# A hybrid decoder layer in float32: the first gate and up pair of each half step done by two plain k groups and seven products

## The chip, the cores and the metric

One core of one Trainium2 chip. The metric is the device time of one execution in microseconds (us), here the median of three runs. Engines: PE (TensorE, matmuls), ACT (ScalarE), DVE (VectorE), POOL (GpSimd) and SP (SyncE, which issues most loads).

## The reference, cut to what matters

One layer on x of 256 tokens x 2048 channels. The two SwiGLU half steps, with which the change deals, are its first and its last part:

```python
x = x + 0.5 * swiglu(rms_norm(x, ffn1_norm[l]), ffn1_w_gate[l], ffn1_w_up[l], ffn1_w_down[l])
x = x + hybrid_mixer(rms_norm(x, mix_norm[l]), ...)
x = x + cross_attention(rms_norm(x, xattn_norm[l]), ...)
x = x + 0.5 * swiglu(rms_norm(x, ffn2_norm[l]), ffn2_w_gate[l], ffn2_w_up[l], ffn2_w_down[l])

def swiglu(h, w_gate, w_up, w_down):
    return (jax.nn.silu(h @ w_gate) * (h @ w_up)) @ w_down
```

w_gate and w_up are 2048 x 5632, w_down is 5632 x 2048, all float32.

## The kernel before, in words

**Numbers.** A float32 matmul is done as three with operands in a reduced float32 form: a value is split into a high part (a cast, on ACT) and a low part (value less high part, on DVE), and high x high, high x low and low x high are added up in PSUM. `split` (L144) does it; `wsplit` does it for weights and keeps the casts, and the low halves, in the order in which they are written.

**Tiles.** Tokens are two tiles (TT) of 128, each the stationary operand of a matmul. A k group is 512 rows of a weight matrix by 512 columns: a raw tile [128, 4, 512] of 1 MB, which `load` (L130) has SP fetch into one of a few places (tag "raw", in a pool `wp` and in the phase's own pool), and from which `wgroup` (L151) makes the split tiles wh and wl. A gate or up column block f (eleven of 512 columns) has four k groups over the 2048 channels: 24 matmuls of 128 x 512 for each group and matrix, in `mm3` (L170) or `whole` (L179). The normed x stands transposed and split in xT[0] to xT[3], one for each k group. The norm's factor r is applied behind the products.

**Seven products.** `strassen` (L223) takes two k groups (a, b), the two token tiles and a pair of matrices (gate and up, or two column blocks of down) and does their eight block products (`product`, L213, twelve matmuls each) as seven. For it DVE adds raw weights (`raw`, L237), a DMA on POOL's queue adds others in memory (L241, accumulating), the sums of x blocks sh and sl are made once by `sums_of` (L198: six steps on DVE in tiles fa and fb, then the split), and the products x and y, made in PSUM, are carried over into accumulators by an ACT copy (L254) and two DVE subtractions (L264, L269). The products in order, with a and b of the k groups, are: x from the left raw a; y from left a less right a (sh, sl); x again with another sum; c0l from the left b; x; c0r; and, behind or inside the whole groups, the seventh from x's second tile.

**A half step** is `ffn` (L374): the eleven f in three parts (4, 4 and 3). For each f the gate and up products, silu on ACT (sg, L420), h on DVE (L428), and, two ticks later, `turn` (L378): four PE transposes (tp, L383) for each token tile and the split of h into hTh (ACT) and hTl (DVE, L303). After a part its rows of w_down, by `strassen` over the part's first two h groups and whole groups for the rest, and x is updated (L442). For f = 0 both matrices are done plainly: `proj` (L288) runs gate over four groups, then up over four; the sums of xT[0] and xT[1] are made behind that. From f = 1 on `strassen` takes k groups 0 and 1 and `whole` does 2 and 3.

**At the start** three raw groups (gate 0, 1, 2) are loaded with x's transposed blocks xr; `first` (L481) multiplies these by the norm's gain (ACT for the first block, POOL for the others, L325), splits them into xTh and xTl. At the end of a half step `norm_chunk` (L334) makes the next phase's operands from each updated block of x: one tick later eight transposes (L343), the multiplication by the gain (xg, L345) and the split (L348, L349).

**What sets the order.** A scheduler gives each engine a fixed order by priorities (`tc.high_priority`, WPRI for weights) ahead of the run; `later` and `tick` (L89 to L100) place transposes a number of products later. Tiles live in pools by tag; a tile whose tag has n places waits for the release of the one n before it. A phase's pool is opened by `open_phase` (L64) and released at the end: half step 1, middle, half step 2. wh and wl have FWB = 3 places of a whole group in a half step and WB = 4 of half a group in the middle.

Of the kernel before, what the change touches and what calls it, by code (L numbers as in the profile page):

```python
# [8 lines left out]
F32 = mybir.dt.float32  # L9
# [7 lines left out]
P = 128  # L17
# [12 lines left out]
WB = 4  # L30
# [19 lines left out]
def layer_kernel(ctx: ExitStack, tc: tile.TileContext, A: dict, out: bass.AP):  # L50
# [65 lines left out]
    with tc.high_priority(100000):  # L116
        SY.dma_start(gain, A["gains"])
        for g in range(3):
            raw = wp.tile([P, 4, 512], F32, tag="raw", name="raw")
            wload.append(raw)  # L120
            step = 2 if g else 1
            xr = FT("h", 8, [P, 4, S], F32, "xr")
            xload.append(xr)
            for k in range(0, 4, step):
                SY.dma_start(xr[:, k:k + step], A["xT"][g, :, k:k + step])
                SY.dma_start(raw[:, k:k + step], A["ffn1_w_gate"][0, g, :, k:k + step])
    xs = [con.tile([P, TT, 512], F32, name=f"x{c}") for c in range(NC)]
# [22 lines left out]

    def wgroup(W, c, g, fine=None):  # L151
# [70 lines left out]

    def strassen(Wl, cl, Wr, cr, lhs, ab, sums, groups, mid=None, last=False):  # L223

# [26 lines left out]
        c0l, c0r, c1r = (pa.tile([P, 512], F32, tag="acc", name="acc") for _ in range(3))  # L251
        product(x, of(a, 0), parts(ral), True)
        with tc.high_priority(WPRI):
            SC.copy(c0l, x)  # L254
        add(ral, ral, rar)
# [6 lines left out]
        product(x, s_(1), parts(ral), False)  # L262
        with tc.high_priority(WPRI):
            V.tensor_sub(c0r, ys, x)  # L264
# [3 lines left out]
        with tc.high_priority(WPRI):  # L268
            V.tensor_sub(c1r, ys, x)  # L269
# [17 lines left out]

    def proj(W, c, lhs, groups, fine=None):  # L288

# [3 lines left out]
        for i, g in enumerate(groups):  # L293
            if fine and i:
                fine(4 * i)
            for h, half in enumerate(wgroup(W, c, g, fine if i == 0 else None)):
# [37 lines left out]
    def norm_chunk(c, src, g0, ss):  # L334
# [15 lines left out]

        later(1, turn)

# [21 lines left out]
    def ffn(pre, r, after, fine=None, last=False):  # L374
# [18 lines left out]
        for part in PARTS:  # L393
# [13 lines left out]
            for f in part:  # L407
                plain = sums is None
                if plain:
                    gate = proj(wg, f, lhs_x, range(4), fine)  # L410
                    if callable(r):
                        r = r()
                else:
                    gate, upv = strassen(wg, f, wu, f, lhs_x, (0, 1), sums, (2, 3),
                                         mid=sums_h if f == part[-1] else None)
                sg = []
# [5 lines left out]
                if plain:  # L422
                    upv = proj(wu, f, lhs_x, range(4))
                hs = []
                with tc.high_priority(WPRI):
                    for t in range(TT):
# [3 lines left out]
                later(2, lambda f=f, hs=hs: turn(f, hs))  # L430
                if plain:
                    with tc.high_priority(WPRI):
                        sums = sums_of(xT[0], xT[1])
                    kept = [tc.dram_tile([P, 2, 4, S], F32, name=f"{pre}_{n}") for n in ("sh", "sl")]
# [647 lines left out]
```

## Time and profile before

| | |
|---|---|
| median of three runs | 1919.73 us (1919.63 to 1920.5) |
| profiled execution | 1920.29 us |
| its span | 1918.5 us, granted clock 0.995 |
| matmuls and transposes | 8616 |
| PE, weight loads, DVE, ACT, POOL busy | 99%, 81%, 76%, 56%, 7% |
| memory read over the span | 379.10 MB |

In rows of waits stand total us, times and the longest wait. In rows of a timeline stand the start, the length, engine, line, operation, out<-in, the count of instructions merged, and in brackets the idle time before it with what ended it. In rows of groups stand the count, total us busy, mean ns of one and idle time before. "acc<-wh,xTh" is a matmul of the split weight and the split x into the accumulator acc.

### The profile page before, as it was taken

How to read it: one execution, taken by the hardware profiler on the slowest of the kernel's cores; microseconds unless marked ns; L12 is line 12 of the kernel's file. 1: busy time of each engine (PE TensorE's matmuls, PEld its weight loads, DVE VectorE, ACT ScalarE, POOL GpSimd, SP SyncE). 2: the span in 40 equal slices, each digit the busy share in tenths (PEclk: the TensorE clock that was granted, in tenths of full speed). 3: DMA queues.
4: the chain of work that ended last, by engine and by line, in shares of the span. 5: the costliest groups of instructions: out<-in, count | busy, mean ns of one | idle time of the engine just before them, and what ended most of it. 6: DMA issues, size and time to landing. Idle time of an engine off the chain costs nothing.

```text
span 1918.5 us, 21566 instructions
## 1 busy us (share of the span) xinstructions
PE 1890.5 (99%) x8616; PEld 1563.4 (81%) x8616; DVE 1459.3 (76%) x1159; ACT 1080.1 (56%) x1028; POOL 125.7 (7%) x137
## 2 busy tenths in 40 slices
PE   8999999999999999999999999899999999999998
PEld 6888888888888778778888889788888888888876
DVE  7779887788888885446785555777888878888886
ACT  6556655555555556444676445555655556556553
POOL 2000000000000000002230000000000000000000
PEclk9999999999999999999999999899999999999999
DMA  9776787777877754445465554668768777787775
GB/s 376 274 244 225 241 301 280 275 240 241 277 246 274 250 157 174 169 158 194 174 221 200 195 193 157 254 198 293 231 230 285 259 275 272 246 284 233 242 253 171
DMA packets 68480, 453.90 MB, mean 237 GB/s; under 512 B 7675, under 2 KB 8827, under 8 KB 15004
## 3 DMA queue, kind: packets, MB, share of 16 engines
q1 hardware_dynamic: 56284, 370.74, 49.2%
q0 software_dynamic: 10944, 79.70, 18.5%
q10 hardware_dynamic: 1152, 2.10, 0.3%
q8 instruction: 67, 1.10, 0.2%
q14 instruction: 33, 0.27, 0.0%
HBM read 379.10 MB, written 6.29 MB: 201 GB/s over the span
## 4 chain that ended last, share of the span: by engine, by line
PE 93%; DVE 4%; issue 1%; ACT 1%; DMA 1%; POOL 0%; SPq 0%; DVEq 0%; POOLq 0%; ACTq 0%
PE acc L184 24%; PE x L219 17%; PE acc L176 9%; PE acc L177 9%; PE acc L175 9%; PE acc L219 9%; PE x L184 8%; PE y L219 4%; DVE wl L145 2%; ACT wh L145 1%; PE tp L383 1%; DVE raw L237 1%; DMA xr<-in_xT_dram 0%; DMA raw<-raw 0%; PE tp L343 0%
## 5 line engine op out<-in xcount | busy, mean ns | idle before, releaser
L145 DVE TENSOR_TENSOR wl<-raw,wh 128x2048 fp32r<-128x2048 f32 (+2 forms) x523 | 1013.6, 1954 | 367.1 <-ACT wh L145 366.7
L145 ACT CAST wh<-raw 128x2048 fp32r<-128x2048 f32 (+2 forms) x523 | 852.2, 1640 | 621.3 <-DVE raw L237 182.2
L175 PE MATMUL acc<-wh,xTh 128*128 128x512 f32 x544 | 216.3, 399 | 9.0 <-ACT wh L145 8.8
L176 PE MATMUL acc<-wl,xTh 128*128 128x512 f32 x544 | 214.9, 395 | 4.6 <-DVE wl L145 4.6
L177 PE MATMUL acc<-wh,xTl 128*128 128x512 f32 x544 | 214.2, 394 | 0.0
L237 DVE TENSOR_TENSOR raw<-raw 128x2048 f32<-128x2048 f32 x64 | 146.5, 2290 | 1.7
L241 POOL DMA_DIRECT2D raw<-raw x64 | 55.0, 860 | 1201.2 <-ACT sg L420 473.8
L175 PEld LDWEIGHTS acc<-wh,xTh 128*128 128x128 f32 x544 | 103.1, 190 | 32.4 <-ACT wh L145 10.5
L176 PEld LDWEIGHTS acc<-wl,xTh 128*128 128x128 f32 x544 | 103.6, 190 | 28.0 <-DVE wl L145 6.9
L184 PE MATMUL acc<-wl,xTh 128*128 128x512 f32 x480 | 121.8, 389 | 0.0
L184 PE MATMUL acc<-wh,xTl 128*128 128x512 f32 x480 | 121.8, 389 | 0.0
L184 PE MATMUL acc<-wh,xTh 128*128 128x512 f32 x480 | 121.8, 389 | 0.0
L177 PEld LDWEIGHTS acc<-wh,xTl 128*128 128x128 f32 x544 | 103.6, 190 | 21.7
L184 PEld LDWEIGHTS acc<-wl,xTh 128*128 128x128 f32 x480 | 90.1, 188 | 18.7
L184 PEld LDWEIGHTS acc<-wh,xTh 128*128 128x128 f32 x480 | 90.1, 188 | 18.7
L184 PEld LDWEIGHTS acc<-wh,xTl 128*128 128x128 f32 x480 | 90.1, 188 | 18.7
L219 PE MATMUL x<-wh,sh 128*128 128x512 f32 x256 | 71.2, 400 | 3.3 <-ACT wh L145 1.9
L219 PE MATMUL x<-wh,sl 128*128 128x512 f32 x256 | 68.8, 390 | 0.0
L219 PE MATMUL x<-wl,sh 128*128 128x512 f32 x256 | 68.7, 390 | 0.0
L420 ACT ACTIVATE sg<-acc,r 128x512 f32<-128x512 f32 x24 | 16.3, 689 | 84.7 <-PE acc L184 84.7
L184 PE MATMUL acc<-wh,hTl 128*128 128x512 f32 x232 | 59.2, 390 | 2.4 <-DVE hTl L303 2.4
L184 PE MATMUL acc<-wh,hTh 128*128 128x512 f32 x232 | 59.2, 390 | 0.9 <-ACT wh L145 0.9
(339 smaller groups left out, 2828.3 us busy)
## 6 DMA issues: line engine op xcount, KB each, us to landing
raw<-in_ffn_w_up_dram SPq DMA_DIRECT2D x88, 1024.0 KB, 8.9
raw<-in_ffn_w_down_dram SPq DMA_DIRECT2D x88, 1024.0 KB, 7.6
raw<-in_ffn_w_gate_dram SPq DMA_DIRECT2D x85, 1024.0 KB, 7.8
raw<-raw POOLq DMA_DIRECT2D x64, 1024.0 KB, 6.9
raw<-in_w_in_dram SPq DMA_DIRECT2D x48, 1024.0 KB, 4.8
raw<-in_w_out_dram SPq DMA_DIRECT2D x16, 1024.0 KB, 4.8
sl<-ffn_sl POOLq DMA_DIRECT2D x4, 1024.0 KB, 9.4
sh<-ffn_sh POOLq DMA_DIRECT2D x4, 1024.0 KB, 13.3
```

The lines of the kernel that those rows point to most:

```text
L145: return SC.copy(wh, src), V.tensor_sub(wl, src, wh.bitcast(F32))
L175: PE.matmul(acc[t], lh, wh, start=first and i == 0, stop=False, skip_group_check=seeded)
L176: PE.matmul(acc[t], lh, wl, start=False, stop=False, skip_group_check=seeded)
L177: PE.matmul(acc[t], ll, wh, start=False, stop=last and i == len(half) - 1, skip_group_check=seeded)
L184: PE.matmul(acc[t], lhs(w[0], t)[i], w[1 + j], start=False, stop=last and j == 1 and n == len(group) - 1, skip_group_check=True)
L219: PE.matmul(acc, lhs(k)[i], w[:, k], start=first, stop=j == 1 and k == 3, skip_group_check=not start)
L237: V.tensor_add(dst, x, y)
L241: G.dma_start(dst, x, accum_op=ALU.add)
L383: PE.transpose(tp[:, j], hs[t][:, j * P:(j + 1) * P], ident)
L420: SC.activation(s, gate[t], AF.Silu, scale=r[:, t:t + 1])
```

## The change

It does five things.

1. For f = 0 of each half step a new function `lead` does gate 0, up 0, gate 1, up 1 plainly (k groups 0 and 1), splitting each group in two halves, the very first in four. Then the sums of xT[2] and xT[3] are made, and `strassen` does k groups 2 and 3 with the four accumulators of `lead` (`ahead`). A product that is carried over there goes to a tile "seed" in SBUF and is added by DVE to the accumulator (`seed`).
2. At the start gate 0, up 0 and gate 1 are loaded, and x's third block later.
3. `open_phase` takes places for wh and wl (in the half steps for raw and h too) ahead of everything else, so that the tiles of all phases have the same places.
4. The transposes of the odd x blocks come two ticks later than those of the even ones.
5. hTh and hTl are split under high priority.

```diff
+        for tag in ("wh", "wl"):
+            if half_step:
+                FT(tag, FWB, [P, 4, 512], F32R, tag)
+            else:
+                FT(tag, WB, [P, 2, 512], F32R, tag)
+        if half_step:
+            FT("raw", FRAW, [P, 4, 512], F32, "raw")
+            FT("h", 8, [P, 4, S], F32, "h")
...
-        for g in range(3):
+        for i, (W, g) in enumerate((("gate", 0), ("up", 0), ("gate", 1))):
...
-                for i in range(m if fine else 1):
-                    d = slice(i, i + 1) if fine else slice(0, m)
+                for i in range(0, m, step or m):
+                    d = slice(i, i + (step or m))
...
+        def seed(acc, src, less=None):
+
+            with tc.high_priority(WPRI):
+                if ahead is None:
+                    if less is None:
+                        SC.copy(acc, src)
+                    else:
+                        V.tensor_sub(acc, src, less)
+                    return
+                s = W2([P, 512], "seed")
+                if less is None:
+                    SC.copy(s, src)
+                else:
+                    V.tensor_sub(s, src, less)
+                V.tensor_add(acc, s, acc)
...
+        if ahead is None:
+            c0l, c0r, c1r = (pa.tile([P, 512], F32, tag="acc", name="acc") for _ in range(3))
+        else:
+            (c0l, c1l), (c0r, c1r) = ahead
...
+        if ahead is not None:
+            product(x, of(b, 1), parts(ral), False)
+            seed(c1l, x)
+            return ahead
...
+    def lead(Wl, cl, Wr, cr, lhs, groups, fine=None):
+
+        accs = tuple(tuple(pa.tile([P, 512], F32, tag="acc", name="acc") for _ in range(TT)) for _ in range(2))
+        for i, g in enumerate(groups):
+            for acc, W, c in zip(accs, (Wl, Wr), (cl, cr)):
+                own = fine if i == 0 and acc is accs[0] else None
+                for h, half in enumerate(wgroup(W, c, g, own, 1 if own else 2)):
+                    mm3(acc, lhs, half, i == 0 and h == 0, i == len(groups) - 1 and h == 1)
+                    tick()
+                if fine and (i or acc is accs[0]):
+                    fine(4 * (i + 1) + 4 * (i and acc is accs[1]))
+        return accs
...
-        later(1, turn)
+        later(1 + 2 * (c % 2), turn)
...
-                split_from_psum(hi[:, :, sl], lo[:, :, sl], tp)
+                with tc.high_priority(WPRI):
+                    split_from_psum(hi[:, :, sl], lo[:, :, sl], tp)
...
-                plain = sums is None
-                if plain:
-                    gate = proj(wg, f, lhs_x, range(4), fine)
+                ahead = None
+                if sums is None:
+                    ahead = lead(wg, f, wu, f, lhs_x, (0, 1), fine)
+                    with tc.high_priority(WPRI):
+                        sums = sums_of(xT[2], xT[3])
...
-                    gate, upv = strassen(wg, f, wu, f, lhs_x, (0, 1), sums, (2, 3),
-                                         mid=sums_h if f == part[-1] else None)
+                gate, upv = strassen(wg, f, wu, f, lhs_x, (2, 3), sums, () if ahead else (0, 1),
+                                     mid=sums_h if f == part[-1] else None, ahead=ahead)
```

From f = 1 on the seven products so take k groups 2 and 3, and 0 and 1 are the whole ones.

**DVE's order, first half step, from the sums of x to the first products.** (The numbers tell tiles of one name apart; in the changed kernel the split is L156, the raw add L249, the sums L215 to L219.) Before, the sums are made between the splits of plain groups, and six splits stand between them and the first raw add:

```order
L145 TENSOR_TENSOR wl_323<-raw_320,wh_322 128x2048
L206 TENSOR_TENSOR fa_446<-fa_446 128x4x128
L207 TENSOR_TENSOR fa_446<-fb_447,fa_446 128x4x128
L208 TENSOR_TENSOR fb_447<-fb_447,fa_446 128x4x128
L145 TENSOR_TENSOR wl_353<-raw_350,wh_352 128x2048
L145 TENSOR_TENSOR sl_445<-fa_446,sh_444 128x1024
L145 TENSOR_TENSOR sl_445<-fb_447,sh_444 128x1024
L145 TENSOR_TENSOR wl_383<-raw_380,wh_382 128x2048
L145 TENSOR_TENSOR wl_413<-raw_410,wh_412 128x2048
L145 TENSOR_TENSOR wl_478<-raw_464,wh_477 128x2048
L237 TENSOR_TENSOR raw_464<-raw_464,raw_466 128x2048
```

In the changed kernel the same place, from the last part of xT[3] on:

```order
L370 TENSOR_TENSOR xTl3_289<-xr_290,xTh3_288 128x512
L215 TENSOR_TENSOR fb_301<-xTh3_288,xTl3_289 128x1024
L216 TENSOR_TENSOR fb_301<-fa_300,fb_301 128x4x128
L156 TENSOR_TENSOR wl_350<-raw_339,wh_349 128x2048
L217 TENSOR_TENSOR fa_300<-fa_300 128x4x128
L249 TENSOR_TENSOR raw_339<-raw_339,raw_341 128x2048
L218 TENSOR_TENSOR fa_300<-fb_301,fa_300 128x4x128
L219 TENSOR_TENSOR fb_301<-fb_301,fa_300 128x4x128
L156 TENSOR_TENSOR wl_371<-raw_339,wh_370 128x2048
L156 TENSOR_TENSOR sl_299<-fa_300,sh_298 128x1024
L156 TENSOR_TENSOR sl_299<-fb_301,sh_298 128x1024
L249 TENSOR_TENSOR raw_339<-raw_339,raw_343 128x2048
```

The sums (fa, fb, sl) now use xT[2] and xT[3], and the first product's split (wl_350), the raw add and the second product's split (wl_371) stand among them, with the second raw add right behind.

**DVE's order, first half step, from the end of f = 0 into f = 1.** Before, f = 1's first product's split (wl_478) is followed at once by its raw add:

```order
L145 TENSOR_TENSOR wl_478<-raw_464,wh_477 128x2048
L237 TENSOR_TENSOR raw_464<-raw_464,raw_466 128x2048
L145 TENSOR_TENSOR wl_497<-raw_464,wh_496 128x2048
L237 TENSOR_TENSOR raw_464<-raw_464,raw_468 128x2048
L363 TENSOR_REDUCE r1t_308<-ss1_287 128x2
L365 TENSOR_SCALAR r1m_310<-r1t_308 128x2
L145 TENSOR_TENSOR wl_532<-raw_464,wh_531 128x2048
```

In the changed kernel, from f = 0's seventh product (wl_461) on:

```order
L156 TENSOR_TENSOR wl_461<-raw_339,wh_460 128x2048
L275 TENSOR_TENSOR seed_441<-ys_386,x_347 128x512
L156 TENSOR_TENSOR wl_507<-raw_493,wh_506 128x2048
L276 TENSOR_TENSOR acc_129<-seed_441,acc_129 128x512
L249 TENSOR_TENSOR raw_493<-raw_493,raw_495 128x2048
L276 TENSOR_TENSOR acc_127<-seed_476,acc_127 128x512
L469 SCALAR_TENSOR_TENSOR h_483<-acc_128,r1_337,sg_479 128x512
L469 SCALAR_TENSOR_TENSOR h_485<-acc_129,r1_337,sg_481 128x512
L156 TENSOR_TENSOR wl_526<-raw_493,wh_525 128x2048
L346 TENSOR_TENSOR hTl_542<-tp_543,hTh_541 128x4x128
L249 TENSOR_TENSOR raw_493<-raw_493,raw_497 128x2048
L346 TENSOR_TENSOR hTl_542<-tp_550,hTh_541 128x4x128
```

Seed steps now stand around f = 1's first split (wl_507) and its raw add, and the first hTl stands ahead of the second raw add, where before hTl came after f = 1's whole groups' splits had begun.

**PE's order, end of the first half step.** x_100 and x_101 are the first two updated blocks of x, L343 their transposes, L219 the products of the last pair of down's column blocks but one. Before:

```order
L219 MATMUL x<-wh,hTh 128x512 x4
L219 MATMUL x<-wh,hTl 128x512 x4
L219 MATMUL x<-wl,hTh 128x512 x4
L343 MATMUL tp<-ident,x_100 128x128 x8
L343 MATMUL tp<-ident,x_101 128x128 x8
L219 MATMUL y<-wh,sh 128x512 x4
```

In the changed kernel the same blocks are x_101 and x_102, the transposes are L386, the products L230 and the whole groups L195; eleven rows from the first product on:

```order
L386 MATMUL tp<-ident,x_101 128x128 x8
L230 MATMUL y<-wh,sh 128x512 x4
L230 MATMUL y<-wh,sl 128x512 x4
L230 MATMUL y<-wl,sh 128x512 x4
L230 MATMUL x<-wh,sh 128x512 x4
L230 MATMUL x<-wh,sl 128x512 x4
L230 MATMUL acc<-wh,hTh 128x512
L230 MATMUL x<-wl,sh 128x512 x4
L230 MATMUL acc<-wh,hTh 128x512 x3
L230 MATMUL acc<-wh,hTl 128x512 x4
L230 MATMUL acc<-wl,hTh 128x512 x4
L195 MATMUL acc<-wh,hTh 128x512 x4
```

The second block's eight transposes have left this run: they stand 12 rows further, inside the whole group behind the fourth product. Those of the third and fourth block stand together ahead of the middle phase, as before.

More of the change, by code (lines that the diff above doesn't have):

```diff
@@ L117, in layer_kernel @@
         SY.dma_start(gain, A["gains"])
[L118 removed]
+        for i, (W, g) in enumerate((("gate", 0), ("up", 0), ("gate", 1))):
             raw = wp.tile([P, 4, 512], F32, tag="raw", name="raw")
             wload.append(raw)
[L121 to L123 removed]
+            step = 2 if i else 1
+            if i != 1:
+                xr = FT("h", 8, [P, 4, S], F32, "xr")
+                xload.append(xr)
             for k in range(0, 4, step):
[L125 to L126 removed]
+                if i != 1:
+                    SY.dma_start(xr[:, k:k + step], A["xT"][g, :, k:k + step])
+                SY.dma_start(raw[:, k:k + step], A[f"ffn1_w_{W}"][0, g, :, k:k + step])
     xs = [con.tile([P, TT, 512], F32, name=f"x{c}") for c in range(NC)]
@@ L149, in wsplit, with wgroup @@
             in_turn(key, ins)
-    def wgroup(W, c, g, fine=None):
+    def wgroup(W, c, g, fine=None, step=None):
         raw = load(W, c, g)
@@ L221, in product, with strassen @@
         tick()
-    def strassen(Wl, cl, Wr, cr, lhs, ab, sums, groups, mid=None, last=False):
+    def strassen(Wl, cl, Wr, cr, lhs, ab, sums, groups, mid=None, last=False, ahead=None):
         a, b = ab
@@ L248, in s_ @@
             return lambda k: tuple(x[:, g, k, t * P:(t + 1) * P] for x in sums)
+        def seed(acc, src, less=None):
[12 more added lines that the diff above has]
+                V.tensor_add(acc, s, acc)
         x, y = PM([P, 512], "x"), PM([P, 512], "y")
-        c0l, c0r, c1r = (pa.tile([P, 512], F32, tag="acc", name="acc") for _ in range(3))
+        if ahead is None:
+            c0l, c0r, c1r = (pa.tile([P, 512], F32, tag="acc", name="acc") for _ in range(3))
+        else:
+            (c0l, c1l), (c0r, c1r) = ahead
         product(x, of(a, 0), parts(ral), True)
-        with tc.high_priority(WPRI):
-            SC.copy(c0l, x)
+        seed(c0l, x)
         add(ral, ral, rar)
@@ L262, in strassen @@
         product(x, s_(1), parts(ral), False)
-        with tc.high_priority(WPRI):
-            V.tensor_sub(c0r, ys, x)
+        seed(c0r, ys, x)
         product(c0l, of(b, 0), parts(rbl), False)
@@ L267, in strassen @@
         product(x, s_(2), parts(rar), False)
-        with tc.high_priority(WPRI):
-            V.tensor_sub(c1r, ys, x)
+        seed(c1r, ys, x)
         product(c0r, s_(3), parts(rbr), False)
@@ L286, in strassen, with proj @@
         return accs
-    def proj(W, c, lhs, groups, fine=None):
+    def proj(W, c, lhs, groups):
         n = W.shape[-1]
@@ L293, in proj @@
         for i, g in enumerate(groups):
-            if fine and i:
-                fine(4 * i)
-            for h, half in enumerate(wgroup(W, c, g, fine if i == 0 else None)):
+            for h, half in enumerate(wgroup(W, c, g)):
                 mm3(acc, lhs, half, i == 0 and h == 0, i == len(groups) - 1 and h == 1)
@@ L430, in ffn @@
                 later(2, lambda f=f, hs=hs: turn(f, hs))
-                if plain:
-                    with tc.high_priority(WPRI):
-                        sums = sums_of(xT[0], xT[1])
+                if ahead:
                     kept = [tc.dram_tile([P, 2, 4, S], F32, name=f"{pre}_{n}") for n in ("sh", "sl")]
```

7 lines of the change are left out of this document (1 added, 6 removed).

## The prediction

> **What bounds the kernel now.** I read the page first: busy shares and the chain that ended last.
>
> ```profile
> PE 1890.5 (99%) x8616; PEld 1563.4 (81%) x8616; DVE 1459.3 (76%) x1159; ACT 1080.1 (56%) x1028; POOL 125.7 (7%) x137
> ...
> PE 93%; DVE 4%; issue 1%; ACT 1%; DMA 1%; POOL 0%; SPq 0%; DVEq 0%; POOLq 0%; ACTq 0%
> ```
>
> TensorE is the bound, with VectorE behind it at three quarters. So an edit is worth what it takes from the matmuls, plus what it does to the few places where PE waits. The view of waits names those for PE, and PE's timeline gives their places.
>
> ```profile
> PE acc L175 <- ACT wh L145: 8.8, 3, 4.4
> PE acc L176 <- DVE wl L145: 4.6, 3, 2.7
> PE acc L184 <- DVE hTl L303: 2.4, 2, 1.5
> PE tp L343 <- DVE xg L345: 1.9, 1, 1.9
> ```
>
> ```profile
> 17.36 0.73 PE L175 MATMUL acc<-wh,xTh 128*128 128x512 f32 x2 [4.40 <-ACT wh L145]
> 19.68 0.80 PE L176 MATMUL acc<-wl,xTh 128*128 128x512 f32 x1 [1.60 <-DVE wl L145]
> ...
> 25.25 0.39 PE L175 MATMUL acc<-wh,xTh 128*128 128x512 f32 x1
> ...
> 665.89 1.19 PE L184 MATMUL acc<-wh,hTl 128*128 128x512 f32 x4 [1.50 <-DVE hTl L303]
> ...
> 682.09 0.66 PE L343 MATMUL tp<-ident,x 128*128 128x128 f32 x4 [1.88 <-DVE xg L345]
> ...
> 1216.80 1.22 PE L175 MATMUL acc<-wh,xTh 128*128 128x512 f32 x2 [3.29 <-ACT wh L145]
> 1220.75 0.79 PE L176 MATMUL acc<-wl,xTh 128*128 128x512 f32 x1 [2.73 <-DVE wl L145]
> ...
> 1868.35 2.11 PE L184 MATMUL acc<-wh,hTh 128*128 128x512 f32 x8 [0.60 <-ACT wh L145]
> 1871.38 1.19 PE L184 MATMUL acc<-wh,hTl 128*128 128x512 f32 x4 [0.92 <-DVE hTl L303]
> ```
>
> The waits stand at the two places where a half step begins (17 to 25 us and 1217 to 1227 us) and at its two ends (666 to 687 us, 1871 us): just where the change works. Between them PE runs without a gap. How much room VectorE has at the two beginnings is in the windows: from the start, and from the first transpose of the second half step (1211.60), to the end of the sixth product of the second gate and up pair, f=1, the first point that both kernels share.
>
> ```profile
> 0.00:78.30 78.30, 69.31 (x293) 55.83 (x294) 56.68 (x45) 49.44 (x60) 15.97 (x20) 0.96 0.83 303
> 1211.60:1284.15 72.55, 66.53 (x290) 54.30 (x289) 52.74 (x40) 39.80 (x34) 4.53 (x5) 0.93 0.69 235
> ```
>
> Columns after the length are PE, PEld, DVE, ACT and POOL busy: VectorE was busy 56.68 of 78.30 us and 52.74 of 72.55 us. Two pieces of the chain of waits end these windows (start and length): twelve matmuls take 2.72 us, 0.2267 each, and the sixth product ends at 78.29 and 1284.15. The third row is the product behind the wait at 682.09.
>
> ```profile
> 75.57 2.72 PE acc L219 x12
> ```
>
> ```profile
> 1281.43 2.72 PE acc L219 x12
> ```
>
> ```profile
> 682.78 4.58 PE y L219 x12
> ```
>
> **The change, part by part.** Prices of what the change adds, by the groups of one form (busy us, mean ns):
>
> ```profile
> L145 DVE TENSOR_TENSOR wl<-raw,wh 128x2048 fp32r<-128x2048 f32 x359 | 814.4, 2289 | 230.5 <-ACT wh L145 230.4
> L145 ACT CAST wh<-raw 128x2048 fp32r<-128x2048 f32 x359 | 682.4, 1913 | 466.5 <-DVE raw L237 182.2 <-PE x L184 83.5 <-PE acc L184 66.7
> ...
> L237 DVE TENSOR_TENSOR raw<-raw 128x2048 f32<-128x2048 f32 x64 | 146.5, 2290 | 1.7
> ...
> L264 DVE TENSOR_TENSOR acc<-ys,x 128x512 f32<-128x512 f32 x32 | 22.0, 688 | 2.0 <-PE x L219 2.0
> ```
>
> *Matmuls.* 180 instead of 192 in the first pair of each half step: 24 fewer in all, 24 x 0.2267 = 5.44 us, half of it in each half step.
>
> *Work for it.* Per half step there are three more groups to split (11 against 8), two adds of raw weights, and six seed operations on VectorE: 3 x 2.29 + 2 x 2.29 + 6 x 0.69 = 15.6 us of VectorE for 2.72 us of PE. ScalarE gets 3 x 1.91 and two copies, with 29 us free in the first window. In the first window VectorE would hold 56.7 + 15.6 = 72.3 of 78.3 us, though much of that work can begin only when the last of x has landed and been multiplied, at 27 us (below). That it has no room there is the core of this forecast. The seeds have no row of their own: from below they would cost nothing (hidden beside products), from above two 128x512 operations each, so I take 0.69 from the nearest row, the subtraction into acc.
>
> *First half step, the lead.* up 0 needs no new part of x, so its 24 matmuls fall into the 4.40 us that PE waited at 17.36. By my timetable from the landings (2 MB landed between the second and third row below, about 2.5 us for each) PE goes through gate 0, up 0, gate 1, up 1 by 30.1 us. Before, 24 matmuls were done ahead of 17.36 and 15 more by 25.25, so the 96th ended at 25.25 + 57 x 0.2267 = 38.2 us. Gain 8.1 us, both waits included.
>
> ```profile
> 17.55 2.98 POOL L325 TENSOR_TENSOR xr<-xr,gain 128x512 f32<-128x512 f32 x1 [0.42 <-DMA xr<-in_xT_dram]
> 22.50 4.49 POOL L325 TENSOR_TENSOR xr<-xr,gain 128x512 f32<-128x512 f32 x2 [1.97 <-DMA xr<-in_xT_dram]
> ```
>
> *First half step, the products.* Here that gain is given back. The second product, y, now needs the sums of xT[2] and xT[3], the last parts of x to arrive, where until now f=1 was the first to need sums, and those of xT[0] and xT[1]. Six MB still go through SP's queue ahead of the last of xT[3], so GpSimd multiplies it until about 27, as in the row of 22.50. Then on VectorE, in the order shown: its low part to 28.2, fb to 30.0, the split of the first product (2.2) and one fa step to 32.8, the raw add to 35.1. ScalarE casts that sum for y first (to 37.0) and sh only then (two casts of about 1, to 38.9); VectorE splits the weights to 39.2 and sl to 41.5. PE ends the first product at 33.1 and waits 5.8 us for sh, then 1.6 for sl: 7.4. The pattern behind each further raw add is in VectorE's timeline, and the accumulating DMA's time to landing in the page's list:
>
> ```profile
> 1841.79 2.28 DVE L237 TENSOR_TENSOR raw<-raw 128x2048 f32<-128x2048 f32 x1
> 1846.10 2.29 DVE L145 TENSOR_TENSOR wl<-raw,wh 128x2048 fp32r<-128x2048 f32 x1 [2.03 <-ACT wh L145]
> ```
>
> ```profile
> raw<-raw POOLq DMA_DIRECT2D x64, 1024.0 KB, 6.9
> ```
>
> 4.31 us from the add's start to the low half's, with VectorE idle for two of them if nothing is queued to fill it. So the third product's weights come at 47.9, and products three to seven run at VectorE's pace (the seventh also waits for the accumulating DMA that GpSimd issues, 6.9 us) to about 61: 5.3 us of waits with that of f=1's first product and the 0.3 at the first one. In f=1 the raw add stands behind the last product's split, a seed subtraction, f=1's first split and a seed add, so f=1's second product waits 3.9; its second raw add stands behind a hTl, which needs the transposes behind that product, so the third waits 4.3. Waits in all: 7.4 + 5.3 + 3.9 + 4.3 = 20.9. End of f=1's sixth product: 30.1 + 156 matmuls x 0.2267 (35.4) + transposes 0.9 + 20.9 = 87.3 against 78.3: **+9.0**. Behind it are whole groups, on which PE is the bound again, so the loss stays. The lower bound is VectorE never idle from 28.2 on: its queue from there to the split of that sixth product (seventeen 128x2048 operations at 2.2 to 2.3 apart, the rest small) adds up to 50 us, and four matmuls stand behind it: 79.1, or +0.8. The upper is the accumulating DMA two us later: +11.
>
> *End of the first half step.* hTl under the high priority takes the 1.50 at 665.89 away, and x0's transposes alone need one PSUM place fewer at a time, which takes away the 1.88 at 682.09 and the 1.86 (4.58 - 2.72) by which the product behind it was slow: 5.2. What comes late instead by the order: eight transposes inside the whole group behind the fourth product, and the next phase's first splits, which now wait for the places of the last products' split tiles: 2.0 for the cast, 1.6 for the low half and 0.6 for the product behind the transposes, by when those places come free in my timetable. I take **-1.0**, between -5 (none of that) and +2.
>
> *Start of the second half step.* Before, gate 0 began 5.2 us after the first transpose (1216.80) and waited 2.73 for its low half (1220.75). Shared places set it at 6.15, lead ends at 31.3 (96 x 0.2267 = 21.8, 1.3 for wl, 2 of slow clock), seven products to 51 (19.0 and 0.7), then f=1's six with transposes 17.2 and the same two waits behind raw adds, 3.9 and 4.3: 76.4 against 72.55: **+3.9**. Bounds: 0 and +6. Weights are there early here, so the 7.4 at y has no counterpart.
>
> *End of the second half step.* The 0.92 at 1871.38 and 0.60 ahead of it go: **-1.5** (-3 to 0).
>
> *Shared places and odd chunks' transposes in the middle.* No wait of PE that they could remove is in the view between 705 and 1200 us: 0.
>
> Sum: 9.0 - 1.0 + 3.9 - 1.5 = **+10.4**, on 1920.29 of the profiled execution (its span is 1918.5, 1.79 less), which lies 0.56 above the median; on the median 1919.73 it gives **1930.1**.
>
> **Rivals.**
>
> *Faster: the bound stays PE.* One mechanism: the second half step's VectorE queue has enough lead (its raw weights lie ready) that both raw adds of f=1 end before PE asks. It decides there with a queue shorter by 4 us. Then that part is 6.15 + 1.3 + 252 x 0.2267 + 0.9 + 2 = 67.5, 5.0 below before; with the lower bound +0.8 in the first, -5 at its end and -1.5: -10.7, **1909.0**. For it: PE's 99% and 19.8 us of idle VectorE in that window. Against: 15.6 of those go to the new work.
>
> The Trainium skill, "Perfetto Trace Analysis", section "Identifying the Most-Contended Engine", says to improve the engine of highest occupancy and to judge TensorE by its weight loads. That rule speaks for this rival, as weight loads are at 81% against VectorE's 76%. By that rule alone the time would come out near 1914, less 5.44.
>
> *About the same: VectorE is full but never idle.* +0.8 in the first part, 0 at the second's start, -1.0 and -1.5: -1.7, **1918.0**. For it: ScalarE and the memory are free enough. Against: the two us of idle behind each raw add above.
>
> *Slower still: half clock behind each new wait.* The product behind the wait of 1.88 took 4.58 instead of 2.72. With that 1.86 on three of the new long waits (y, and f=1's in both half steps): +5.6, **1935.7**. Against: the wait of 1.50 at 665.89 has its four matmuls in 1.19, unslowed, and where VectorE sets the pace a slower clock is hidden.
>
> The Trainium skill, "TensorE: Matmul & The Clock Gate", Part 1's table, puts the fall to half clock behind an idle window of about 3.4 us. The trace shows it behind 1.88 us, shorter than that, so I don't go by the page.
>
> *The change doesn't do what it says:* the transposes of x2 and x3 still stand in one run ahead of both following phases, so "apart" holds for x0 and x1 alone. That is in the -1.0 already.
>
> **How the numbers follow.** Forecast 0.62, its own range 1924 to 1936 (the bounds of the four terms, not all at once); slower still 0.11; about the same 0.14; faster 0.13. A measurement of this kernel tells about 0.2%, 3.8 us, from no change. Faster by more than that: the faster rival and a little of the same one, 0.15; within: 0.14; slower: 0.71. The range leaves out the faster rival and the far end of the slower: 1916 to 1937.
>
> **What would show it.** Right: no wait at the second group near 17 us, PE in up 1 by 30 us; a wait of 5 to 8 us at y's first matmul for sh and sl; waits of about 4 at L230 in f=1 behind raw adds; the window to f=1's sixth product of 85 to 89 us with VectorE busy over 70. Wrong: y's wait below 2 us, or f=1's sixth product before 80 us; 1.50 and 1.88 still there at the half step's end; a wait in the middle from shared places.

## The result, and the profile after

| | before | changed |
|---|---|---|
| median | 1919.68 us (4 runs, 1918.78 to 1920.5) | 1933.65 us (4 runs, 1932.95 to 1934.48) |
| span of the profiled execution | 1918.5 us | 1931.8 us |
| ratio, 95% interval | | 1.0073 (1.0056 to 1.0091) |

The changed kernel is 14 us slower, and the interval of the ratio lies clear of 1. The page of its profile, busy time and the chain that ended last:

```profile
PE 1891.7 (98%) x8592; PEld 1561.4 (81%) x8592; DVE 1491.5 (77%) x1188; ACT 1095.6 (57%) x1047; POOL 126.8 (7%) x141
...
PE 91%; DVE 3%; ACT 2%; DMA 2%; issue 1%; POOL 0%; SPq 0%; ACTq 0%; DVEq 0%
```

There are 24 matmuls fewer, and PE is busy for 1.2 us longer: its records are longer where its clock is lower. From 40.81 to 47.30 us the granted clock was 0.50, and four matmuls stand in the timeline with 2.07 us; from 59.08 to 73.20 it was 1.00, and four stand with 1.07. The waits of its PE by cause (total us, times, longest):

```profile
PE x L230 <- ACT seed L273: 7.0, 1, 7.0
PE x L230 <- ACT wh L156: 6.2, 4, 3.5
PE acc L186 <- ACT wh L156: 5.9, 2, 4.3
PE y L230 <- ACT sh L156: 5.0, 1, 5.0
PE y L230 <- ACT wh L156: 3.9, 2, 3.5
PE acc L195 <- ACT wh L156: 2.5, 1, 2.5
```

Before, the list was led by waits of the plain groups for their splits. Now four of the six rows are seven-product products (L230), of the new pair and of f=1 behind it, and one row is a wait that the forecast's sum did not have: for a seed copy on ACT, 7.0 us in one piece. PE's timeline has the places (start, length, idle before):

```profile
34.11 1.67 PE L230 MATMUL x<-wl,xTh 128*128 128x512 f32 x4 [1.79 <-DVE wl L156]
40.81 2.07 PE L230 MATMUL y<-wh,sh 128*128 128x512 f32 x4 [5.04 <-ACT sh L156]
43.52 2.08 PE L230 MATMUL y<-wh,sl 128*128 128x512 f32 x4 [0.63 <-DVE sl L156]
54.26 2.07 PE L230 MATMUL x<-wh,sh 128*128 128x512 f32 x4 [6.96 <-ACT seed L273]
...
73.23 1.20 PE L230 MATMUL y<-wh,sh 128*128 128x512 f32 x4 [0.39 <-ACT wh L156]
76.81 1.21 PE L230 MATMUL y<-wl,sh 128*128 128x512 f32 x4 [0.59 <-DVE wl L156]
81.54 1.36 PE L230 MATMUL x<-wh,sh 128*128 128x512 f32 x4 [3.52 <-ACT wh L156]
...
703.02 1.60 PE L195 MATMUL acc<-wh,hTh 128*128 128x512 f32 x4 [2.48 <-ACT wh L156]
...
1231.07 1.22 PE L186 MATMUL acc<-wh,xTh 128*128 128x512 f32 x2 [4.26 <-ACT wh L156]
...
1262.27 1.21 PE L230 MATMUL x<-wh,sh 128*128 128x512 f32 x4 [1.15 <-ACT wh L156]
...
1283.86 2.07 PE L230 MATMUL y<-wh,sh 128*128 128x512 f32 x4 [3.54 <-ACT wh L156]
```

Gone are the wait of 4.40 at the second group, and at the half steps' ends those of 1.50, 1.88 and 0.92. The window from the start to the end of f=1's sixth product is now 94.65 us long, against 78.30:

```profile
0.00:94.65 94.65, 72.98 (x281) 56.89 (x282) 75.87 (x62) 57.41 (x69) 15.77 (x22) 0.84 0.81 276
```

Granted clock 0.84, against 0.96 before. How far the changed kernel is behind at points that both have (VectorE's rows of h and x in its timeline; behind f=10 PE's row, as VectorE's two rows of h for f=10 stand together before, and 2.86 us apart in the changed kernel):

| row | before | changed | behind |
|---|---|---|---|
| first h of f=1, first half step | 103.52 | 119.87 | +16.35 |
| PE's first product of down behind f=10 | 642.07 | 657.71 | +15.64 |
| last update of x, first half step | 711.92 | 725.00 | +13.08 |
| first h of f=1, second half step | 1309.37 | 1327.44 | +18.07 |
| PE's first product of down behind f=10 | 1847.85 | 1865.27 | +17.42 |
| last update of x | 1914.25 | 1927.46 | +13.21 |

So the two starts cost 16.35 and 18.07 - 13.08 = 5.0 us, the two ends give back 15.64 - 13.08 = 2.6 and 17.42 - 13.21 = 4.2, and the pairs and parts between, where nothing was forecast, give back 0.7 in each half step.

Where the 16.35 come from can be added up from PE's records: idle between its instructions went from 7.93 to 20.61 (+12.7); the time between starts of 128x512 matmuls beyond 0.227 us, outside gaps, from 3.76 to 9.65 (+5.9); twelve matmuls fewer are -2.7. That makes 15.9; the rest, half a microsecond, is not accounted for.

### The profile page after: what moved, and what is told of

Its sections match the earlier page's. It is cut to its first block, busy times and chain, and to the rows that moved or that the text cites. A ratio compares the mean times of both kernels' runs of the same rounds, so it can differ in the third digit from the quotient of the medians.

```text
span 1931.8 us, 21588 instructions
## 1 busy us (share of the span) xinstructions
PE 1891.7 (98%) x8592; PEld 1561.4 (81%) x8592; DVE 1491.5 (77%) x1188; ACT 1095.6 (57%) x1047; POOL 126.8 (7%) x141
## 4 chain that ended last, share of the span: by engine, by line
PE 91%; DVE 3%; ACT 2%; DMA 2%; issue 1%; POOL 0%; SPq 0%; ACTq 0%; DVEq 0%
PE acc L195 25%; PE x L230 18%; PE acc L230 9%; PE x L195 8%; PE acc L187 8%; PE acc L188 8%; PE acc L186 8%; PE y L230 4%; ACT wh L156 1%; DVE raw L249 1%; DVE wl L156 1%; PE tp L426 1%; DMA raw<-raw 1%; DMA xr<-in_xT_dram 1%; PE tp L386 0%
## 5 line engine op out<-in xcount | busy, mean ns | idle before, releaser
L156 DVE TENSOR_TENSOR wl<-raw,wh 128x2048 fp32r<-128x2048 f32 (+2 forms) x536 | 1027.3, 1936 | 350.9 <-ACT wh L156 350.3
L156 ACT CAST wh<-raw 128x2048 fp32r<-128x2048 f32 (+2 forms) x536 | 863.5, 1624 | 621.9 <-DVE raw L249 198.3
L186 PE MATMUL acc<-wh,xTh 128*128 128x512 f32 x480 | 190.6, 399 | 6.0 <-ACT wh L156 5.9
L187 PE MATMUL acc<-wl,xTh 128*128 128x512 f32 x480 | 188.8, 393 | 0.4 <-DVE wl L156 0.3
L188 PE MATMUL acc<-wh,xTl 128*128 128x512 f32 x480 | 188.4, 392 | 0.0
L249 DVE TENSOR_TENSOR raw<-raw 128x2048 f32<-128x2048 f32 x68 | 155.7, 2290 | 1.8
L195 PE MATMUL acc<-wh,xTh 128*128 128x512 f32 x480 | 122.0, 389 | 0.0
L195 PE MATMUL acc<-wl,xTh 128*128 128x512 f32 x480 | 121.8, 389 | 0.0
L195 PE MATMUL acc<-wh,xTl 128*128 128x512 f32 x480 | 121.8, 389 | 0.0
L186 PEld LDWEIGHTS acc<-wh,xTh 128*128 128x128 f32 x480 | 90.6, 189 | 26.0 <-ACT wh L156 6.7
L187 PEld LDWEIGHTS acc<-wl,xTh 128*128 128x128 f32 x480 | 91.2, 190 | 20.2 <-DVE wl L156 1.7
L188 PEld LDWEIGHTS acc<-wh,xTl 128*128 128x128 f32 x480 | 91.1, 190 | 19.2
L195 PEld LDWEIGHTS acc<-wh,xTh 128*128 128x128 f32 x480 | 90.1, 188 | 18.7
L195 PEld LDWEIGHTS acc<-wl,xTh 128*128 128x128 f32 x480 | 90.1, 188 | 18.7
L195 PEld LDWEIGHTS acc<-wh,xTl 128*128 128x128 f32 x480 | 90.1, 188 | 18.7
L230 PE MATMUL x<-wh,sh 128*128 128x512 f32 x272 | 76.7, 404 | 13.2 <-ACT seed L273 7.0
L230 PE MATMUL x<-wh,sl 128*128 128x512 f32 x272 | 74.8, 397 | 0.0
L230 PE MATMUL x<-wl,sh 128*128 128x512 f32 x272 | 74.0, 394 | 0.2 <-DVE wl L156 0.2
L230 PEld LDWEIGHTS x<-wh,sh 128*128 128x128 f32 x272 | 48.7, 190 | 25.7 <-ACT wh L156 7.7
L195 PE MATMUL acc<-wh,hTh 128*128 128x512 f32 x232 | 59.5, 391 | 2.5 <-ACT wh L156 2.5
```

The costliest lines, as they stand in the source:

```text
L156: return SC.copy(wh, src), V.tensor_sub(wl, src, wh.bitcast(F32))
L186: PE.matmul(acc[t], lh, wh, start=first and i == 0, stop=False, skip_group_check=seeded)
L187: PE.matmul(acc[t], lh, wl, start=False, stop=False, skip_group_check=seeded)
L188: PE.matmul(acc[t], ll, wh, start=False, stop=last and i == len(half) - 1, skip_group_check=seeded)
L195: PE.matmul(acc[t], lhs(w[0], t)[i], w[1 + j], start=False, stop=last and j == 1 and n == len(group) - 1, skip_group_check=True)
L230: PE.matmul(acc, lhs(k)[i], w[:, k], start=first, stop=j == 1 and k == 3, skip_group_check=not start)
```

## The experiments

Theory D is the forecast's: VectorE has no room, and sets the pace of the products. Theory C was formed from the row at 54.26: the products are held by the place of single instructions in ScalarE's order. Theory A and B ask which part of the change does what.

The kernel before, run on the same chip, had medians of 1919.44 (e1 to e4), 1918.65 (e5 to e8) and 1918.71 us (e9 to e12).

| run | time, us | ratio to before, 95% interval |
|---|---|---|
| e1 first pair plain, rest kept | 1912.49 | 0.9966 (0.9953 to 0.9979) |
| e2 new pair alone | 1942.13 | 1.0117 (1.0100 to 1.0134) |
| e3 seed copy in turn, squares later | 1934.79 | 1.0078 (1.0062 to 1.0093) |
| e4 all four groups alternating, plain | 1916.52 | 0.9985 (0.9976 to 0.9995) |
| e5 sums of the early x blocks | 1932.06 | 1.0067 (1.0052 to 1.0082) |
| e6 seed copy alone earlier | 1932.36 | 1.0068 (1.0053 to 1.0083) |
| e7 e4 with x loaded earlier | 1907.47 | 0.9936 (0.9922 to 0.9951) |
| e8 shared places alone | 1919.42 | 1.0002 (0.9992 to 1.0011) |
| e9 no low halves in the new products | 1935.53 | 1.0082 (1.0067 to 1.0097) |
| e10 high priority of hT alone | 1918.95 | 0.9999 (0.9990 to 1.0009) |
| e11 odd transposes later alone | 1917.20 | 0.9988 (0.9979 to 0.9998) |
| e12 e1 with x loaded earlier | 1915.76 | 0.9982 (0.9973 to 0.9991) |

**e1 and e2: which part costs and which gains.** e1 takes the new pair out of the changed kernel:

```diff
-                if sums is None:
-                    ahead = lead(wg, f, wu, f, lhs_x, (0, 1), fine)
+                plain = sums is None
+                if plain:
+                    gate = proj(wg, f, lhs_x, range(4), fine)
...
-                gate, upv = strassen(wg, f, wu, f, lhs_x, (2, 3), sums, () if ahead else (0, 1),
+                    gate, upv = strassen(wg, f, wu, f, lhs_x, (0, 1), sums, (2, 3),
```

> The first pair of each half step as before (four plain k groups of gate, then of up, and the loads in the old order); shared places, transposes of the odd blocks two ticks later and hTh, hTl under high priority are kept. Theory A (the new pair causes the whole loss, the other parts gain by themselves what the ledger shows behind the pairs, 2.5 us at the first half step's end, 4.2 at the second's, about 1.5 in between): 1910 to 1913 us. Theory B (the other parts gain only beside the new pair, or shared places cost something at the starts): 1918 us or more.

1912.49. e2 does the reverse, and puts `lead`, `seed` and the pair with its loads into the kernel before.

> The kernel before with the new pair and its loads alone. Theory A: the losses of the two starts, 16.4 and about 4 us, without the gains: 1938 to 1941 us. Theory B (shared places and later transposes cause the loss at the second start, and gain nothing): 1932 to 1936 us.

1942.13. The pair alone costs 22.7 us, and the rest alone gains 7.0. e1 lies within theory A's range, e2 1.1 us above it and far from theory B's: the pair causes the loss. In e2 the waits at the start are those of the changed kernel within a few tenths (5.20, 6.96, 3.52), and those of the ends (1.51, 1.88, 0.91) are back.

**e3 and e6: the seed copy.** In the changed kernel ScalarE's timeline ahead of 54.26 reads:

```profile
45.77 5.50 ACT L156 CAST wh<-raw 128x2048 fp32r<-128x2048 f32 x3 [2.54 <-DVE raw L249]
51.18 0.63 ACT L375 ACTIVATE junk<-x 128x512 f32<-128x512 f32 x1
...
53.65 0.56 ACT L273 COPY seed<-x 128x512 f32<-128x512 f32 x1
```

The third product adds onto x in PSUM, so it needs the first product to be copied out of x (L273). That product had ended by 36, but the copy stands behind the casts of the third, fourth and fifth product (45.77 to 51.27) and, behind these, four squares of x (L375), and starts at 53.65. e3 puts it ahead of the fourth product's cast, and the squares behind the pair:

```diff
+                    if acc is c0l:
+                        in_turn("cast", ins)
...
-        product(x, s_(1), parts(ral), False)
+        third = parts(ral)
+        if ahead is not None:
+            seed(c0l, x)
+        product(x, s_(1), third, False)
...
-                    if callable(r):
-                        r = r()
```

> The changed kernel with ScalarE's copy of the first product into its seed tile put ahead of the fourth product's cast, and with the squares of x behind the pair; nothing is left out. Theory C (the 6.96 us before the third product are ScalarE's order: the copy stands behind three casts, one of which waits for an accumulating DMA, and behind four of the squares): that wait falls below 2 us, and 1926 to 1929 us. Theory D (as forecast: VectorE has no room, so what is won at the third product is lost again by its splits): 1931 us or more.

1934.79: the third product's wait fell to 1.16, as theory C has it, but the total did not fall. In its PE timeline:

```profile
44.66 2.07 PE L230 MATMUL y<-wh,sh 128*128 128x512 f32 x4 [11.50 <-ACT sh L156]
...
52.12 1.19 PE L230 MATMUL x<-wh,sh 128*128 128x512 f32 x4 [1.16 <-ACT seed L273]
```

Moving the squares changed more than I wanted: the scheduler put the third product's cast between the two casts of sh, so that y's wait grew from 5.04 to 11.50. Its time is within theory D's range, but with y starting 3.9 us later it decides nothing between C and D. e6 leaves the squares alone, and moves the copy only (the first two pieces of the diff above).

> The changed kernel; only the first seed copy on ScalarE is moved, from behind the casts of the third, fourth and fifth product to behind that of the third (four squares of x and the copy ys still stand ahead of it). Theory C: the copy ends about 3 us earlier, the third product's wait falls from 6.96 to about 4, and f=1's end and the total fall by 2.5 to 3 us, to about 1931 us. Theory D: no change over 1 us.

```profile
50.96 2.07 PE L230 MATMUL x<-wh,sh 128*128 128x512 f32 x4 [3.84 <-ACT seed L273]
...
1260.78 2.07 PE L230 MATMUL x<-wh,sh 128*128 128x512 f32 x4 [2.14 <-ACT seed L273]
```

The wait fell by 3.1, and f=1's h came at 117.26 instead of 119.87, 2.6 earlier: theory C's number, and nothing of it was lost again in the first half step. In the second one the third product now waits 2.14 for a seed copy, where it waited 1.15 for a cast; so the total fell by less, to 1932.36 (runs from 1929.79 to 1934.14). Those runs overlap with the changed kernel's, and the ratios to before, 1.0068 and 1.0073, are the same within their intervals: theory C is shown by the trace of the first start, and not by the total.

**e5: are the sums late, or is VectorE full?**

```diff
-                        sums = sums_of(xT[2], xT[3])
+                        sums = sums_of(xT[0], xT[1])
```

> The changed kernel with the sums made from the first and second x block in place of the third and fourth (same instructions, and the products use these other sums, so the values are not the reference's). Theory D (as forecast: the sums come late, and VectorE's queue then sets the pace): the waits of 5.04 and 0.63 at y fall to about 2, and the total falls by about as much or a little more, to 1928 to 1930 us. Theory C (behind y the third product waits for ScalarE's late seed copy, at about 52 us whenever y starts): what y wins is lost there, the third product's wait grows from 6.96 to 9 us or more, and the total falls by 2 us or less, to 1931.5 to 1933.5 us.

1932.06, within theory C's range, but only half for its reason. The third product starts at 54.27, as it did at 54.26, with a wait of 7.79 where theory C had 9 or more. Yet y did not start earlier either:

```profile
40.99 2.08 PE L230 MATMUL y<-wh,sh 128*128 128x512 f32 x4 [4.75 <-ACT wh L156]
```

With sh early (its casts end at 36.7), y waits for its weights instead: VectorE's queue ran without idle to the end of the raw add, at 38.9. Up to this point of the start theory D fits: that y is late is due to VectorE's queue, not to the arrival of x alone.

**e9: take VectorE's new work away.**

```diff
+                if ahead is not None:
+                    wh = FT("wh", FWB, [P, 4, 512], F32R, "wh")
+                    in_turn("cast", SC.copy(wh, src))
+                    return wh, wh
```

> The changed kernel without the low halves of the weights in the seven products of the first pair: their matmuls run on the high half in its place, so that VectorE has 7 x 2.29 = 16 us less in each half step, about what the change gave it, and PE as many matmuls (values are not the reference's). Theory D (VectorE has no room): the loss of the two starts, 16.4 and about 4 us, nearly goes: 1918 us or less. Theory C (the chain raw add, cast, seed copy on ScalarE holds the products, full VectorE or not): the third product still waits 6 us or more for the seed copy, which still stands behind casts and squares, and the total is 1924 to 1930 us.

1935.53 (runs from 1932.49, the profiled one, to 1936.73): no gain from 16 us less of VectorE in each half step, which neither theory had. (At the first start it lost another 1.8 us, f=1's h at 121.72; the second start cost 2.3 us instead of 5.0.) VectorE's, ScalarE's and PE's rows of the same place, one kernel, three timelines:

```profile
56.12 0.16 DVE L410 TENSOR_REDUCE r1t<-ss 128x2 f32<-128x8 f32 x1 [15.02 <-ACT junk L379]
```

```profile
54.75 0.63 ACT L379 ACTIVATE junk<-x 128x512 f32<-128x512 f32 x1 [4.93 <-DMA x<-in_x_dram]
...
55.99 0.56 ACT L277 COPY seed<-x 128x512 f32<-128x512 f32 x1
```

```profile
38.45 2.08 PE L230 MATMUL y<-wh,sh 128*128 128x512 f32 x4 [5.57 <-ACT sh L156]
...
56.60 2.07 PE L230 MATMUL x<-wh,sh 128*128 128x512 f32 x4 [11.68 <-ACT seed L277]
```

VectorE stands idle for 15.02 us, and PE waits 11.68 for the seed copy, which stands behind all eight squares; the last two of these wait 4.93 us for x's fourth block to be loaded. So at the first start a free VectorE is not enough: the copy, and what stands ahead of it, set when the third product begins. Of the second start's loss the load explains about half. What VectorE's work costs by itself at the first start e9 doesn't tell: y started 2.4 us earlier than in the changed kernel (38.45 for 40.81), but x's fourth block landed later, at 54.7, where it had landed by 50.3 (issued at 28.18, at most 22.1 to landing). ScalarE's order is: while the copy stands behind the squares, the third product can't begin before x has landed, however free VectorE is. That theory D has no say once the copy stands elsewhere is not shown: no run had both the copy early and the squares out of its way without moving something else. The changed kernel with x loaded earlier wasn't tried.

**e4, e7 and e12: keep the alternating order, leave the seven products.** e4 does all four k groups of f = 0 in `lead`, gate and up in turn, as 192 plain matmuls:

```diff
-                    ahead = lead(wg, f, wu, f, lhs_x, (0, 1), fine)
+                    ahead = gate, upv = lead(wg, f, wu, f, lhs_x, range(4), fine)
...
```

> The changed kernel with all four k groups of the first pair plain, in the new alternating order gate, up, gate, up; no seven products there, so 24 more matmuls in all, three splits, two raw adds and six seeds fewer in each half step; sums of the third and fourth x block made behind the pair. If the 8 us that the alternating order gains by 30 us are real and nothing behind gives them back: 1903 to 1907 us. If f=1's sums or splits give them back: 1910 to 1913 us.

1916.52, outside both: what the order gained was lost at one place that I had not named.

```profile
70.55 1.97 PE L426 MATMUL tp<-ident,h 128*128 128x128 f32 x8 [12.48 <-DVE h L468]
```

Gate and up now end together, h needs the norm's factor r, and r needs the squares of x; on ScalarE the last four stood behind a cast that waited for an accumulating DMA (issued at 49.72, landed at 63.32). e7 adds one number to e4, the priority of x's loads:

```diff
-XPRI = 170
+XPRI = 300
```

> The kernel with all four k groups led plainly, with the loads of x for the norm's factor at a higher priority (300 for 170). There PE waited 12.48 us at the first transposes of h, since the squares of x, and so the factor, stood behind a cast that waits for an accumulating DMA. If the factor alone was late: that wait falls below 2 us and the total from 1916.5 to 1904 to 1907 us. If the memory is the bound of the start (the loads of x then push the weights back): waits of several us appear at the third and fourth group, and 1911 us or more.

1907.47, 0.5 above the first of its two ranges, 11 us faster than the kernel before (ratio 0.9936, 0.9922 to 0.9951) and the fastest here. About 7 of the 11 are the other parts' (e1). Apart from one of 1.81 in the last part of down, at 682.69, PE's only wait over 0.6 us between the first 10 us and the first half step's end is

```profile
61.56 1.21 PE L230 MATMUL x<-wh,sh 128*128 128x512 f32 x4 [2.57 <-ACT wh L156]
```

and the first h of f=1 comes at 99.57 (103.52 before, 102.61 in e1). To see whether x's earlier load did this alone, e12 has the same number in e1.

> The first experiment (first pair plain and in the old order, the other parts kept) with the loads of x at priority 300 for 170, to tell apart what the alternating order and the earlier x gained in the seventh. If the alternating order gains: no better than the first experiment, 1912 us or more. If the earlier x gains by itself: 1908 us or less.

1915.76, no better than e1: there x's loads go ahead of the third block of xT (GpSimd multiplies it from 23.28, in e1 from 21.73), and PE waits 2.40 us, at 34.71, for a low half that VectorE's order has behind the sums; e1 has no wait there. So the alternating order, with its loads, gains, and needs x early for it.

**e8, e10, e11: the other parts one at a time**, each put alone into the kernel before.

> The kernel before with the shared places of the split tiles alone. As forecast: no gain in the middle, and up to 2 us later at the phases' starts: 1918.5 to 1921 us. If the places cause the gain of 7 us of the first experiment: 1914 us or less.

> The kernel before with the high priority for hTh and hTl alone. As the ledger shows behind the pairs: no waits of 1.50 and 0.92 for hTl and no small ones in the later parts: 3 to 5 us less, 1914 to 1917 us.

> The kernel before with the transposes of the odd x blocks two ticks later alone. It takes the wait of 1.88 at the first half step's end and the slow product behind it, 3 to 4 us less in all, 1915 to 1917 us; if that wait moves instead of going, 1918 us or more.

1919.42, 1918.95 and 1917.20: nothing, nothing, and 1.5 us, where the three together gain 7 (e1). Shared places do nothing by themselves, as forecast. e10 and e11 missed their ranges, e10 by 2 us and e11 by 0.2. The high priority gains something where it was expected to (0.8 and 0.6 us over the pairs and parts of the two half steps, measured on PE from the end of f=1 to the first product of down behind f=10, and the waits for hTl are gone), but loses 4.6 us at the first half step's end:

```profile
677.08 1.36 PE L219 MATMUL x<-wh,sh 128*128 128x512 f32 x4 [2.01 <-ACT wh L145]
...
688.55 1.08 PE L343 MATMUL tp<-ident,x 128*128 128x128 f32 x4 [4.11 <-DVE xg L345]
```

The transposes of two x blocks in one run now wait 4.11 for xg instead of 1.88. In e11, with the blocks apart, no wait stands at them, but the waits for hTl are still there (1.46 at 666.16). So it fits that the two edits gain in full only together; no run had these two without the shared places.

## Why the prediction was right, and where its reasons were not

The time was forecast at 1930.1 and measured at 1933.65, slower as forecast. By its steps:

- *The lead.* Forecast: PE through gate 0 to up 1 by 30.1 us. Measured: the last of its matmuls starts at 30.09 and the first product at 30.32:

```profile
30.09 0.39 PE L188 MATMUL acc<-wh,xTl 128*128 128x512 f32 x1
30.32 1.09 PE L230 MATMUL x<-wh,xTh 128*128 128x512 f32 x4
```

- *The wait at y.* Forecast 5.8 + 1.6 for sh and sl; measured 5.04 + 0.63, with 1.79 ahead of it at the first product where 0.3 was forecast: 7.46 against 7.7 in all.
- *Products three to seven.* "Products three to seven run at VectorE's pace", 5.3 us of waits with f=1's first. This step failed. One wait of 6.96 stands there, for the seed copy in ScalarE's order, and from 54.26 to the end of f=1's first product PE waits for nothing, VectorE included. I had that copy among the things that are hidden (29 us free on ScalarE) and did not look at what stands ahead of it in its queue, and at what these wait for. "That it has no room there is the core of this forecast" is right up to y (e5), and not for the products behind it: e9 took their splits off VectorE and gained nothing.
- *f=1.* Forecast 3.9 and 4.3 behind the raw adds. Measured 0.39 + 0.59 and 3.52: the first raw add had time while PE was late.
- *The sum of the waits* came to 18.9 with these, against 20.9. It was close by luck: one wait too small (5.0 for 6.96, the 0.3 being counted above) and one too large (3.9 for 0.39 + 0.59) nearly made up for each other.
- *Half clock* was left out of the forecast and kept as a rival, 5.6 us, of which 3.7 at the first start. It came, and larger: it is the first start's largest miss. The product behind the wait of 6.96 took 4.98 us where 2.72 is full speed, as a piece of the chain:

```profile
54.26 4.98 PE x L230 x12
```

From 30.32 to 94.65 the granted clock was 0.79, and PE was busy for 45.35 us, where the sum had 35.4 + 0.9: about 9 us more. With waits 2.0 shorter than forecast and the lead 0.2 later, that is the way from +9.0 to +16.35. (Against before the clock costs only +5.9, since the kernel before had a slow stretch of its own, with granted clock 0.57 from 17.36 to 25.25.) The rival that had it named 1935.7, nearer to the measured time than the forecast. Its counterargument, that a slower clock is hidden where VectorE sets the pace, did not hold: behind 54.26 VectorE did not set the pace.

The Trainium skill, "TensorE: Matmul & The Clock Gate", Part 1, has the clock fall behind an idle window of about 3.4 us. Here the waits of 6.96, 5.04 and 3.54 are followed by four matmuls in 2.07, as the page has it; after 0.39 and 1.15 there are four in 1.20 and 1.21, near the 1.07 of full speed. But the waits of 1.79 and 2.48, shorter than the page's window, have slow ones behind them too (1.67 and 1.60, at granted clocks of 0.65 and 0.60), while in e6 a wait of 1.85 has four in 1.21. The trace agrees for the long waits, and a shorter one may or may not be followed by half clock.

- *End of the first half step.* -1.0 forecast, -2.6 measured, with the wait of 2.0 for the next cast at its place (2.48). *Second start.* +3.9 forecast, +5.0 measured; the wait of 3.54 for y is the forecast 3.9, that of 4.3 behind the next raw add came to 1.10. *End of the second.* -1.5 forecast, -4.2 measured: the waits of 0.92 and 0.60 are gone, and that of 1.86 at the last pair fell to 0.41 too. *Between.* 0 forecast, -1.4 measured in the two half steps, in no single row of the list of waits; e10, with the high priority alone, has the same 1.4 there.

So the total came as near as it did in part by luck: the two starts were 8.5 us worse than forecast, and the ends and the stretches between 5.7 us better.

The rival on the other side, faster by 11, had +0.8 at the first start and -5.0 at the second, and failed at both (+16.35 and +5.0).

## What to carry to other kernels

A fixed order is a queue for each engine: when work is added, ask of each new instruction not only how long it takes and whether its engine has room, but which instructions stand ahead of it and what each of these waits for. Here PE waited 7 us for a copy of 0.56. ScalarE's share of busy time, 57%, does not show that; PE's list of waits did, and a run with the suspected load taken off VectorE did not shorten it. Price a wait with what follows it, too: here PE ran slowly behind the long ones.

A product saved on the engine that bounds the kernel was priced at 2.7 us in each half step, and was lost several times over. The order of the loads and the plain groups, with no product saved, brought about as much as both: e7 is 5 us faster than e1 (0.9936 of before, for 0.9966).

## What the runs showed that I had not expected

An accumulating DMA of 1 MB takes 6.9 us in the median of before, but 10.29 (37.18 to 47.47) in the changed kernel's start and 13.6 (49.72 to 63.32) in e4's. The core's DMA engines were busy throughout there (share 1.04 and 0.99), where they have 0.76 from 100 to 640 us of the kernel before. And of three edits that alone gain nothing, nothing and 1.5 us, all three together gained 7.
